# Seven down products spread over two pairs: order, leads and pages of a hand-planned transformer layer

## The chip, the cores and the metric

The kernel runs on one core of one Trainium2 chip. The metric is the device time in microseconds (us) of one execution, as the median of several runs.

## The reference

One layer of a streaming encoder on 512 tokens of width 1024, everything in float32:

```python
x = layer_norm(ALPHA * x + 0.5 * swiglu(x, ffn1_wg, ffn1_wu, ffn1_wd), ln1_g, ln1_b)     # D_FF = 2816
h = x @ w_in                       # q, k, v, indexer (qi, ki, wi), conv gates (bg, cg, u)
attn = dsa_attention(...)          # indexer scores, top 128 keys of each query, softmax with ALiBi over them
conv = bg * causal_dwconv3(cg * u)
x = layer_norm(ALPHA * x + concat(attn, conv) @ w_out, ln2_g, ln2_b)
x = layer_norm(ALPHA * x + 0.5 * swiglu(x, ffn2_wg, ffn2_wu, ffn2_wd), ln3_g, ln3_b)
x = x + sigmoid(x @ ple_gate_w) * (p @ ple_proj_w)

def swiglu(x, wg, wu, wd):
    return (silu(x @ wg) * (x @ wu)) @ wd
```

## The kernel before

**Numbers in two parts.** Every float32 operand of a matmul is split into a high part (a ScalarE cast, L115) and a low part (the rest, a VectorE subtraction, L116), and each product is made of three passes: high by high, high by low, low by high. For the weights of the down projection the low part is made otherwise (`Down.parts`): ScalarE writes the negated rounded value into the low page (L299), a DMA issued from GpSimd's queue adds the raw value to it in memory (L300), and ScalarE casts the high part (L301).

**Pairs.** The hidden width is 22 chunks of 128. In each FFN two chunks are computed plainly; the other twenty are taken two at a time as ten pairs (numbers 1 to 10) with a scheme of seven block products where the plain way has eight (`Two`, L426 to 481). Each product is 24 matmuls of 256 columns (L444). The operands of a pair are made in five steps of `weights` (L388): the load of four raw pages, A11, then S1/S2 (L403, L404), S3/S4 (L410, L411), and A12/A22 (`a2`). The products share two banks: x_ takes product 0, is copied out by ScalarE (L466) into a page `e`, and product 2 is then added onto the same bank; y_ likewise with product 1 (L468). At a pair's end its two chunks are split and summed by `pair_ops` (L269 to 282), whose sums go through the page `s_`.

**Down products.** Two pairs make a group of four chunks. A group's down projection is again seven block products (`Down`, L284 to 368) of 12 matmuls of 512 columns (L339), each with a weight operand of its own, made in this order by `prep`: B11, T1 = B12 - B11, T2 = B22 - T1, T3 = B22 - B12, B22, T4 = B21 - T2, B21. The differences are VectorE's (L305). The results are added into `nat` (L346). There are four such groups; the last six chunks go plainly (L586 to 597), fused with the norm.

**The order.** `order` lists the pair products and down products with an estimated duration (2.9 and 2.7 us), and `begin` lists the loads and preparations with a lead: each is called before the first product whose planned start is at or past the planned start of its own product less the lead. For a group, the down products are those of the pairs before it, and they stand behind certain of its pair products (L552, L553). A program that knows the dependences then orders each engine's queue by this program order and by readiness in a model of its own.

**Pages.** Nearly every operand lives in one of `NPAGES` SBUF pages of 4 KB per partition. `page()` takes the page that has been free longest, `free()` puts it at the end of the list. Both happen in program order; on the chip, the first instruction that writes a page waits for the last one that used it under its former owner, DMAs included.

**Middle.** After the first norm the value blocks (`v_proj`) are computed: the first `NV` at once, the others as fillers between the steps of the top-k search (`choose`). The ALiBi distances `dm` are made by GpSimd (L747, L748) and VectorE (L749).

Of the kernel before, what the change touches and what calls it, by code (L numbers as in the profile page):

```python
# [7 lines left out]
F32 = mybir.dt.float32  # L8
F32R = mybir.dt.float32r
AF = mybir.ActivationFunctionType  # L10
ALU = mybir.AluOpType

P = 128
# [3 lines left out]
NTB = S // P  # L17
# [8 lines left out]
BIG = 1.0e30  # L26
NEG = -1.0e38
REPL = -3.0e38

NPAGES = 41  # L30
BANKS = ((0, 1), (4, 5), (6,), (7, 2, 3))
AHEAD = 25
AHEAD_N = 150
# [2 lines left out]
AHEAD_D2 = 0  # L36


LEAD_L, LEAD_S, LEAD_DL, LEAD_DS = 16.0, 8.0, 18.0, 13.0
T_PLAIN, T_PAIR, T_DOWN = 11.5, 2.9, 2.7  # L40
NEMB = 2
AHEAD_P = 150
NV = 1
NQK = 3
NCH = 20
NPRE = 1
# [16 lines left out]
TOFF = (0, 128, 384, 768, 1280)  # L63
# [3 lines left out]
def layer_kernel(ctx: ExitStack, tc: tile.TileContext, x, ln1_g, ln1_b, ffn1_wg, ffn1_wu, ffn1_wd, w_in,  # L67
                 conv_w, w_out, ln2_g, ln2_b, ffn2_wg, ffn2_wu, ffn2_wd, ln3_g, ln3_b, ple_gate_w, ple_proj_w, x_t, p_t, out):
    nc = tc.nc
    sb = ctx.enter_context(tc.tile_pool(name="sb", bufs=1))  # L70
# [7 lines left out]
    def count(kind):  # L78
        counts[kind] = counts.get(kind, 0) + 1
        return counts[kind] - 1  # L80

    def ring(kind, n, shape, dt=F32):
        i = count(kind)
        return sb.tile(shape, dt, tag=f"{kind}{i % n}", name=f"{kind}_{i}")


    free_pages = list(range(NPAGES))
    owner = {}

    def page(shape, dt=F32R):  # L90
        i = free_pages.pop(0)
        t = sb.tile(shape, dt, tag=f"pg{i}", name=f"pg{i}_{count('pg')}")
        owner[id(t)] = (i, t)
        return t

    def free(*tiles):
        for t in tiles:
            free_pages.append(owner.pop(id(t))[0])
# [4 lines left out]
    def bank(group):  # L103
        g = GROUPS[group]
        return pp.tile([P, 512], F32, tag=f"bk{g[count('bank' + group) % len(g)]}", name=f"bk_{count('bank')}")
# [62 lines left out]
    def ts(t):  # L168
        return slice(t * P, (t + 1) * P)
# [78 lines left out]
    def ffn(X, wg, wu, wd, ln_g, ln_b, first, load_nat, groups, nplain, ahead, ahead_f, ahead_d):  # L248
# [249 lines left out]
        def add_down(f0, pairs):  # L498
            u = Down(f0, pairs)
            prods = u.products()  # L500
            loads = {0: ((0, 0),), 1: ((0, 1),), 2: ((1, 1),), 5: ((1, 0),)}
            for i in range(7):
                for at in loads.get(i, ()):
                    begin.append((LEAD_DL, len(order), lambda at=at: u.load(*at)))
                begin.append((LEAD_DS, len(order), lambda i=i: u.prep(i)))
                order.append((T_DOWN, lambda: next(prods)))
                yield
# [30 lines left out]
        def chain_pairs(pairs):  # L538
            for n in pairs:
                if n < 2 * n_down:  # L540
                    yield from add_pair(2 * n, lambda m, n=n: place_in(n, m), lambda n=n: ops[n // 2].append(pair_ops(pair_of[n])))
                else:
                    yield from add_pair(2 * n, lambda m, n=n: late_place(n, m), lambda n=n: late_done(n))
# [5 lines left out]
        for g in range(n_down):  # L549
            pairs = (2 * g + 2, 2 * g + 3) if g < n_down - 1 else (2 * g + 2, 2 * g + 3, 2 * g + 4)  # L550
            downs = add_down(4 * g, ops[g])
            for i, _ in enumerate(chain_pairs(pairs)):  # L552
                if i >= 2 and i % 3 != 1:  # L553
                    next(downs, None)
            for _ in downs:
                pass
# [75 lines left out]
    with tc.high_priority(offset=10000), tc.manual_schedule():  # L632
# [16 lines left out]
        ps = bank("all")  # L649
# [20 lines left out]
    def colT(u, group, tok0=0, m=P):  # L670

        ps = bank(group)
        mm(ps[:m, :S - tok0], [((u[0][:, c], u[1][:, c]), (x1T[0][:, c, tok0:], x1T[1][:, c, tok0:])) for c in range(NDC)])
        free(*u)
        return ps[:, :S - tok0]

    def col_unit(c0, ahead):
        return unit(rows(w_in[:, c0:c0 + P], 0, NDC), [P, NDC, P], ahead)


    v = []
    wv = [unit(rows(w_in[:, C_V:C_V + 512], c * P, 2), [P, 2, 512], AHEAD_V) for c in range(0, NDC, 2)]

    def v_proj(blocks):
        for t in blocks:
            ps = bank("main")
            mm(ps, [((x1T[0][:, c, ts(t)], x1T[1][:, c, ts(t)]), (wv[c // 2][0][:, c % 2], wv[c // 2][1][:, c % 2])) for c in range(NDC)])
            v.append(page([P, NH, 2, HD]))
            split(v[t][:, :, 0], v[t][:, :, 1], ps.rearrange("p (h d) -> p h d", h=NH))
            if t == NTB - 1:  # L690
                for u in wv:
                    free(*u)
            yield

    for _ in v_proj(range(NV)):
        pass
# [17 lines left out]
    def mm64(ps, q, e, at, k_hi, k_lo):  # L714

        nc.tensor.matmul(ps, lhsT=q[:, e, at], rhs=k_hi, start=True, stop=False)  # L716
        nc.tensor.matmul(ps, lhsT=q[:, e, at], rhs=k_lo, start=False, stop=True)  # L717
# [3 lines left out]
    ps = colT(u, "main", m=72)  # L721
# [12 lines left out]
    for j in range(4):  # L734
        ps = colT(col_unit(C_QI + j * P, AHEAD_I), "main", tok0=P)
# [2 lines left out]
        qi.append(t_)  # L738


    dm_pages = [page([P, 768], F32), page([P, 512], F32)]
    dm = [dm_pages[t // 3][:, TOFF[t % 3]:TOFF[t % 3] + (t + 1) * P] for t in range(NTB)]
    for t in range(NTB):
        w_ = (t + 1) * P
        d = dm[t]
        dn = ring("a", 2, [P, 512])
        nc.gpsimd.iota(d, pattern=[[1, w_]], base=-t * P, channel_multiplier=-1, allow_small_or_imprecise_dtypes=True)  # L747
        nc.gpsimd.tensor_scalar(dn[:, :w_], d, -1.0, None, op0=ALU.mult)  # L748
        nc.vector.tensor_tensor(d, d, dn[:, :w_], op=ALU.min)  # L749
    nc.vector.memset(dm[0][0:64, 64:128], -BIG)  # L750


    sc = {}
    for t in range(1, NTB):
        w_ = (t + 1) * P
        sc[t] = page([P, 512], F32)
        for h in (0, 2, 4, 6, 1, 3, 5, 7):
            ps = bank("sc")
# [10 lines left out]
    def choose():  # L769
        m8 = {t: ring("m8", 3, [P, 8]) for t in sc}  # L770
        for k in range(TOPK // 8):
            for t in sc:
                w_ = (t + 1) * P
                nc.vector.max(m8[t], sc[t][:, :w_])
            for t in sc:
                w_ = (t + 1) * P
                nc.vector.match_replace(sc[t][:, :w_], m8[t], sc[t][:, :w_], REPL)
            yield
        for t in sc:
            w_ = (t + 1) * P  # L780
            d = dm[t]
            nc.vector.tensor_scalar(sc[t][:, :w_], sc[t][:, :w_], REPL, -BIG, op0=ALU.not_equal, op1=ALU.mult)
            nc.vector.tensor_add(d, d, sc[t][:, :w_])
        free(*sc.values())
# [7 lines left out]
    def conv():  # L792
        for j in range(4):
            ps = colT(col_unit(C_CG + j * P, AHEAD_C), "main")
            z = page([P, 514], F32)
            nc.vector.memset(z[:, 0:2], 0.0)
            nc.scalar.copy(z[:, 2:], ps)
            yield
            ps = colT(col_unit(C_U + j * P, AHEAD_C), "main")
            nc.vector.tensor_mul(z[:, 2:], z[:, 2:], ps)  # L800
            y = ring("hf", 2, [P, 512])
            nc.scalar.activation(y, z[:, 0:512], AF.Copy, scale=cw[:, j, 0:1])
            for k in (1, 2):
                nc.vector.scalar_tensor_tensor(y, z[:, k:k + 512], cw[:, j, k:k + 1], y, op0=ALU.mult, op1=ALU.add)
            free(z)
            yield
            ps = colT(col_unit(C_BG + j * P, AHEAD_C), "main")
            nc.vector.tensor_mul(y, y, ps)
            t_ = page([P, 2, 512])
            split(t_[:, 0], t_[:, 1], y)  # L810
            convT.append(t_)
            yield
# [39 lines left out]
    def chain(*gens):  # L852
        for g in gens:
            yield from g

    def pull(g, n=1):
        for _ in range(n):
            next(g, None)

    ch = choose()  # L860
    fill = chain(v_proj(range(NV, NTB)), conv(), *[qk_proj(j, "main") for j in range(NQK)])
    done = 0
    for i in range(NTB - NV + 12 + 2 * NQK):
        while done < min(TOPK // 8 + 1, (i + 1) * (TOPK // 8 + 1) / NCH):
# [10 lines left out]
    def softmax(h):  # L875

        j, e = h // 2, h % 2
        slope = 2.0 ** -(h + 1)
        sp = [page([P, 768], F32), page([P, 512], F32)]
        a = [sp[t // 3][:, TOFF[t % 3]:TOFF[t % 3] + (t + 1) * P] for t in range(NTB)]  # L880
        soft[h] = a, sp
        st = ring("ss", 2, [P, NTB, 3])
        for t in range(NTB):
            w_ = (t + 1) * P
            ps = bank("qk")
            mm64(ps[:, :w_], qT[j], e, ts(t), kT[j][:, e, :w_], kL[j][:, e, :w_])
            nc.vector.tensor_tensor_reduce(a[t], ps[:, :w_], dm[t], -slope, 3.0e38, ALU.add, ALU.min, st[:, t, 0:1])
            nc.scalar.activation(a[t], a[t], AF.Exp, bias=st[:, t, 0:1], scale=-1.0, accum_out=st[:, t, 1:2])
            nc.vector.reciprocal(st[:, t, 2:3], st[:, t, 1:2])
            nc.vector.tensor_scalar(a[t], a[t], st[:, t, 2:3], None, op0=ALU.mult)  # L890
# [45 lines left out]
        if h % 2:  # L936
            free(qT[h // 2], kT[h // 2], kL[h // 2])
    pull(fill, 100)
    free(*v, *dm_pages)


    g_t, b_t = bcast(ln2_g[0]), bcast(ln2_b[0])
# [2 lines left out]
    for t in range(NTB):  # L945
        stats = ring("st", 4, [P, 2, 6])
        for half in range(2):
            hs = slice(half * 512, (half + 1) * 512)
            ps = bank(OB[t])
# [20 lines left out]
    for t in range(NTB):  # L970
# [3 lines left out]
        for half in range(2):  # L974
            cuts = (0, 512) if (t, half) != (NTB - 1, 1) else (0, 256, 512)
            for c0, c1 in zip(cuts, cuts[1:]):
                hs = slice(half * 512 + c0, half * 512 + c1)
                n = c1 - c0
                ps = bank("all")
# [34 lines left out]
```

## Time and profile before

| | |
|---|---|
| median of 3 runs | 1077.49 us |
| lowest and highest run | 1072.87 and 1077.82 us |
| the profiled execution | 1072.63 us |
| its span, first to last instruction | 1070.4 us |
| TensorE, matmuls | 1003.4 us busy, 94% of the span |
| VectorE | 838.8 us, 78% |
| ScalarE | 550.7 us, 51% |
| mean granted TensorE clock | 0.976 of full speed |

The span is that of the one execution that was profiled; durations and idle times below are of that execution. The first FFN lies at about 0 to 390 us, attention and conv from there to about 650, the second FFN to about 1027, and the last gate behind it.

### The profile page before, as it was taken

The page shows a single profiled execution, that of the slowest core. Times are in us where ns is not written, and L with a number is a line of the kernel's source. Part 1 is how long each engine was busy: PE and PEld are TensorE (multiplying, and loading weights), DVE is VectorE, ACT ScalarE, POOL GpSimd, SP SyncE. Part 2 cuts the span into 40 slices and gives each one's busy share as a digit, 9 for nine tenths or more (in the row PEclk, how much of TensorE's full clock was granted, in tenths as well). Part 3 has the DMA queues.
Part 4 walks back from the last instruction along what each step waited for, and adds up shares of the span by engine and source line. Part 5 has one row for each costly group of instructions (what it writes and reads, how often), then busy time and mean ns, then how long its engine had stood idle before and what let it go on. Part 6 is the DMA issues. An engine that isn't in the chain of part 4 may idle for free.

```text
span 1070.4 us, 15655 instructions
## 1 busy us (share of the span) xinstructions
PE 1003.4 (94%) x6215; PEld 896.3 (84%) x6215; DVE 838.8 (78%) x1321; ACT 550.7 (51%) x767; POOL 74.9 (7%) x91
## 2 busy tenths in 40 slices
PE   9997997979998989999999899997997979999998
PEld 7996996979998768888878779996996969988787
DVE  7986886778976866999479889976986778888742
ACT  6655654656655235422576835655654656656111
POOL 0010000100000120000000011000000100000100
PEclk9998998999999999999999999998998999999999
DMA  9575446745657112333102513475546744656121
GB/s 311 143 192 142 116 121 175 195 102 138 155 150 240 55 44 60 89 96 91 40 4 95 192 65 119 119 196 138 133 107 173 188 127 119 155 155 242 41 88 49
DMA packets 108824, 138.14 MB, mean 129 GB/s; under 512 B 6992, under 2 KB 83024, under 8 KB 108752
## 3 DMA queue, kind: packets, MB, share of 16 engines
q1 hardware_dynamic: 100688, 107.79, 31.9%
q0 software_dynamic: 8064, 29.36, 14.3%
q8 instruction: 48, 0.79, 0.3%
q14 instruction: 24, 0.20, 0.1%
HBM read 103.59 MB, written 4.19 MB: 101 GB/s over the span
## 4 chain that ended last, share of the span: by engine, by line
PE 50%; issue 24%; DMA 12%; DVE 8%; ACT 3%; POOL 2%; SPq 0%; POOLq 0%; DVEq 0%; ACTq 0%
PE bk L136 24%; PE bk L444 16%; PE bk L339 7%; DMA pg<-pg 6%; DVE pg L116 3%; DMA pg<-in_ffn_wg_dram 2%; ACT pg L115 2%; DMA pg<-in_ffn_wd_dram 2%; POOL pg L300 2%; DMA pg<-in_w_out_dram 1%; DVE nat L166 1%; PE bk L716 1%; POOL mv L164 1%; PE bk L150 1%; PE bk L717 1%
## 5 line engine op out<-in xcount | busy, mean ns | idle before, releaser
L115 ACT CAST pg<-pg 128x1024 fp32r<-128x1024 f32 (+2 forms) x270 | 254.3, 962 | 236.1 <-DVE pg L116 56.9
L116 DVE TENSOR_TENSOR pg<-pg,pg 128x1024 fp32r<-128x1024 f32 (+2 forms) x270 | 294.8, 1112 | 94.3 <-ACT pg L115 50.7
L444 PE MATMUL bk<-xq,pg 128*128 128x256 f32 x1920 | 244.8, 285 | 5.9 <-ACT pg L479 3.4
L444 PEld LDWEIGHTS bk<-xq,pg 128*128 128x128 f32 x1920 | 240.3, 193 | 11.3 <-ACT pg L479 3.8
L339 PE MATMUL bk<-pg,pg 128*128 128x512 f32 x672 | 176.3, 412 | 40.4 <-DMA pg<-pg 40.4
L339 PEld LDWEIGHTS bk<-pg,pg 128*128 128x128 f32 x672 | 130.1, 201 | 66.9 <-DMA pg<-pg 41.6
L444 PE MATMUL bk<-pg,pg 128*128 128x256 f32 x1440 | 184.1, 283 | 1.1 <-ACT pg L466 1.1
L444 PEld LDWEIGHTS bk<-pg,pg 128*128 128x128 f32 x1440 | 178.9, 192 | 3.6 <-ACT pg L466 1.5
L136 PE MATMUL bk<-pg,pg 128*128 128x512 f32 (+1 forms) x624 | 141.8, 378 | 3.5 <-DVE pg L116 1.7
L136 PE MATMUL bk<-xT,pg 128*128 128x512 f32 (+2 forms) x600 | 134.6, 384 | 0.2 <-ACT xT L115 0.2
L136 PEld LDWEIGHTS bk<-pg,pg 128*128 128x128 f32 x624 | 108.8, 188 | 24.8 <-DVE pg L116 2.5
L136 PEld LDWEIGHTS bk<-xT,pg 128*128 128x128 f32 (+1 forms) x600 | 110.7, 187 | 22.2 <-issue 1.3
L346 DVE SCALAR_TENSOR_TENSOR nat<-bk,nat 128x512 f32<-128x512 f32 x112 | 76.6, 687 | 20.5 <-PE bk L339 19.6
L300 POOL DMA_DIRECT2D pg<-pg x56 | 49.2, 878 | 536.7 <-ACT pg L299 336.0
L301 ACT CAST pg<-pg 128x1024 fp32r<-128x1024 f32 x56 | 58.3, 1045 | 33.8 <-PE bk L444 28.4
L136 PE MATMUL bk<-pg,xT 128*128 128x512 f32 (+1 forms) x312 | 69.3, 374 | 0.0
L299 ACT ACTIVATE pg<-pg 128x1024 fp32r<-128x1024 f32 x56 | 58.6, 1058 | 14.1 <-DVE pg L305 14.1
L136 PEld LDWEIGHTS bk<-pg,xT 128*128 128x128 f32 x312 | 55.1, 188 | 9.7
L164 POOL TENSOR_TENSOR mv<-mv,mhalf 128x1 f32<-128x1 f32 x12 | 18.0, 1497 | 408.9 <-DVE mv L163 408.9
L305 DVE TENSOR_TENSOR pg<-pg,pg 128x1024 f32<-128x1024 f32 x32 | 39.0, 1218 | 1.6 <-PE bk L444 1.5
L453 ACT ACTIVATE a<-pg 128x512 f32<-128x512 f32 x40 | 25.1, 627 | 26.8 <-DVE pg L476 26.8
L136 PEld LDWEIGHTS bk<-xq,pg 128*128 128x128 f32 x288 | 35.7, 192 | 3.7 <-ACT pg L115 1.6
(114 smaller groups left out, 864.1 us busy)
## 6 DMA issues: line engine op xcount, KB each, us to landing
pg<-pg POOLq DMA_DIRECT2D x56, 512.0 KB, 5.7
pg<-in_ffn_wd_dram SPq DMA_DIRECT2D x44, 512.0 KB, 4.6
pg<-in_ffn_wu_dram SPq DMA_DIRECT2D x43, 512.0 KB, 7.0
pg<-in_ffn_wg_dram SPq DMA_DIRECT2D x43, 512.0 KB, 4.8
pg<-in_w_in_dram SPq DMA_DIRECT2D x28, 512.0 KB, 3.6
pg<-in_w_out_dram SPq DMA_DIRECT2D x8, 512.0 KB, 3.9
pg<-in_ple_gate_w_dram SPq DMA_DIRECT2D x8, 512.0 KB, 4.2
pg<-in_x_t_dram SPq DMA_DIRECT2D x8, 256.0 KB, 5.9
```

The lines of the kernel that those rows point to most:

```text
L115: nc.scalar.copy(hi, src)
L116: nc.vector.tensor_sub(lo, src, hi.bitcast(F32))
L136: nc.tensor.matmul(ps, lhsT=st[a], rhs=mv[b], start=first and i == 0 and k == 0, stop=last and i == n - 1 and k == 2)
L164: nc.gpsimd.tensor_tensor(mv[:, 3:4], mv[:, 2:3], mhalf, op=ALU.pow)
L299: nc.scalar.mul(lo, src, -1.0)
L300: nc.gpsimd.dma_start(lo, src, accum_op=ALU.add)
L301: nc.scalar.copy(hi, src)
L305: nc.vector.tensor_sub(t, self.raw[a], self.raw[b])
L339: nc.tensor.matmul(banks[b], lhsT=st[x_][:, SLOT[a], ts(b)], rhs=w[y_][:, i], start=first and i == 0 and n == 0, stop=i == 1 and n == 2, s ...
L346: nc.vector.scalar_tensor_tensor(dst, banks[b], CY, dst, op0=ALU.mult, op1=ALU.add)
L444: nc.tensor.matmul(ps[:, i], lhsT=w[x_][:, c], rhs=X.q[b][y_][:, c], start=first and i == 0 and c == 0 and k == 0, stop=i == 1 and c == 3 ...
L453: nc.scalar.activation(s_t, e[:, :, 0], AF.Silu)
```

## The change

The down products no longer stand behind two of every three pair products but behind every second; the leads change (pair loads 16 to 14, down loads 18 to 22, down preparations 13 to 17; the pairs' other steps stay at 8); there is one page fewer, since `dm` gets a tile of its own (1280 columns) and gives back the two pages that it held from the indexer to the end of attention. `NV` becomes 2: the second value block is computed right behind the first norm, not as a filler.

```diff
-NPAGES = 41
+NPAGES = 40
...
-LEAD_L, LEAD_S, LEAD_DL, LEAD_DS = 16.0, 8.0, 18.0, 13.0
+LEAD_L, LEAD_S, LEAD_DL, LEAD_DS = 14.0, 8.0, 22.0, 17.0
 T_PLAIN, T_PAIR, T_DOWN = 11.5, 2.9, 2.7
...
-NV = 1
+NV = 2
...
             for i, _ in enumerate(chain_pairs(pairs)):
-                if i >= 2 and i % 3 != 1:
+                if i >= 2 and i % 2 == 0:
                     next(downs, None)
             for _ in downs:
                 pass
...
-    dm_pages = [page([P, 768], F32), page([P, 512], F32)]
-    dm = [dm_pages[t // 3][:, TOFF[t % 3]:TOFF[t % 3] + (t + 1) * P] for t in range(NTB)]
+    dm = sb.tile([P, 1280], F32, name="dm")
     for t in range(NTB):
         w_ = (t + 1) * P
-        d = dm[t]
+        d = dm[:, TOFF[t]:TOFF[t + 1]]
...
-    nc.vector.memset(dm[0][0:64, 64:128], -BIG)
+    nc.vector.memset(dm[0:64, 64:128], -BIG)
...
-            d = dm[t]
+            d = dm[:, TOFF[t]:TOFF[t + 1]]
...
-            nc.vector.tensor_tensor_reduce(a[t], ps[:, :w_], dm[t], -slope, 3.0e38, ALU.add, ALU.min, st[:, t, 0:1])
+            nc.vector.tensor_tensor_reduce(a[t], ps[:, :w_], dm[:, TOFF[t]:TOFF[t + 1]], -slope, 3.0e38, ALU.add, ALU.min, st[:, t, 0:1])
...
-    free(*v, *dm_pages)
+    free(*v)
```

## Rows read from the trace of the kernel before

**Rows 1.** The page, busy time of two engines: us (share of the span) xinstructions.

```profile
PE 1003.4 (94%) x6215; PEld 896.3 (84%) x6215; DVE 838.8 (78%) x1321; ACT 550.7 (51%) x767; POOL 74.9 (7%) x91
```

**Rows 2.** Waits: engine, line, whom it waited for: us in total, times, longest.

```profile
PE bk L339 <- DMA pg<-pg: 40.4, 6, 7.1
```

**Rows 3.** Timeline of TensorE, 126 to 176 us: start, us, what [idle before <-releaser].

```profile
141.00 3.04 PE L444 MATMUL bk<-xq,pg 128*128 128x256 f32 x24
143.88 2.91 PE L339 MATMUL bk<-pg,pg 128*128 128x512 f32 x12
146.63 3.04 PE L444 MATMUL bk<-pg,pg 128*128 128x256 f32 x24
...
149.50 2.91 PE L339 MATMUL bk<-pg,pg 128*128 128x512 f32 x12
...
163.62 0.63 PE L339 MATMUL bk<-pg,pg 128*128 128x512 f32 x2
...
171.90 4.43 PE L339 MATMUL bk<-pg,pg 128*128 128x512 f32 x10 [6.50 <-DMA pg<-pg]
```

**Rows 4.** Windows: busy us (x) of PE, PEld, DVE, ACT, POOL; PEclk, DMA share, GB/s.

```profile
103.40:171.90 68.50, 62.00 (x421) 57.66 (x421) 52.52 (x73) 37.61 (x46) 6.09 (x7) 0.95 0.58 144
...
405.00:540.00 135.00, 134.84 (x616) 111.58 (x615) 110.13 (x240) 54.05 (x83) 0.00 (x0) 1.00 0.27 75
...
162.00:178.00 16.00, 9.50 (x52) 8.28 (x52) 7.36 (x9) 5.14 (x7) 1.73 (x2) 0.79 0.83 218
```

**Rows 5.** Timeline of the other engines and SP's queue, 146 to 176 us.

```profile
155.32 0.59 ACT L466 COPY pg<-bk 128x512 f32<-128x512 f32 x1 [0.93 <-PE bk L444]
...
157.33 1.22 DVE L305 TENSOR_TENSOR pg<-pg,pg 128x1024 f32<-128x1024 f32 x1
...
158.46 1.22 DVE L116 TENSOR_TENSOR pg<-pg,pg 128x1024 fp32r<-128x1024 f32 x1
...
160.04 0.92 SPq L394 DMA_DIRECT2D pg<-in_ffn_wg_dram  x2
...
160.58 2.01 ACT L299 ACTIVATE pg<-pg 128x1024 fp32r<-128x1024 f32 x2
...
162.05 1.81 POOL L300 DMA_DIRECT2D pg<-pg  x2 [17.96 <-ACT pg L299]
...
171.88 1.83 DVE L116 TENSOR_TENSOR pg<-pg,pg 128x1024 fp32r<-128x1024 f32 x2 [6.49 <-DMA pg<-pg]
```

**Rows 6.** Timelines of VectorE, GpSimd and TensorE, first FFN's last group, around T4.

```profile
287.86 1.22 DVE L305 TENSOR_TENSOR pg<-pg,pg 128x1024 f32<-128x1024 f32 x1
...
290.93 0.88 POOL L300 DMA_DIRECT2D pg<-pg  x1 [11.41 <-ACT pg L299]
...
300.19 2.91 PE L339 MATMUL bk<-pg,pg 128*128 128x512 f32 x12
```

**Rows 7.** DMA issues, first 142 to 156, then whole span: KB, us to landing.

```profile
pg<-pg POOLq DMA_DIRECT2D x1, 512.0 KB, 4.5
...
pg<-in_ffn_wd_dram SPq DMA_DIRECT2D x44, 512.0 KB, 4.6
```

**Rows 8.** Timeline at the first norm's last block, 376 to 400 us.

```profile
380.26 5.60 PE L136 MATMUL bk<-pg,xT 128*128 128x512 f32 x24
...
382.00 0.95 DVE L749 TENSOR_TENSOR pg<-pg,a 128x384 f32<-128x384 f32 x1 [0.47 <-POOL a L748]
...
389.36 1.09 PE L150 MATMUL bk<-ident,nat 128*128 128x128 f32 x8 [3.50 <-DVE nat L166]
...
390.69 9.18 PE L136 MATMUL bk<-xT,pg 128*72 128x512 f32 x34 [0.24 <-ACT xT L115]
```

## The prediction, made before the change was run

> **What bounds the kernel now.** First the page: TensorE is busy for 94% of the span, no other engine over 78% [rows 1]. So time is to be had where TensorE waits, and at its lowered clock. Second, the waits, longest first: of its 67 us without work, 40.4 lie in six waits of the down projection's matmuls (L339) for one kind of DMA, `pg<-pg`, the accumulating one of L300 that makes a low part [rows 2]. Third, the timeline around the second of the six. I call a group's pair products p0 to p6 (first pair) and q0 to q6 (second), its down products d0 to d6; the next group's are r0 and so on. The third line of [rows 3] is p6, the fourth d3, the last two d5. It multiplies by T4, starts at 163.62, stops after the matmuls that need only the high part, and goes on at 171.90, with its ten remaining matmuls in 4.43 us where twelve take 2.91 (d3). The windows say why: granted clock 0.79 over 16 us, so some of it at the lower level of 1.2 GHz [rows 4]. One group lasts 68.5 us [rows 4]; its work is 14 x 2.88 + 7 x 2.75 = 59.6 (starts in [rows 3]). The stall therefore costs 8.9 us, 6.7 of waiting and some 2.2 of clock, and six cost 53 us.
>
> Why is T4 late? Followed back through the other engines [rows 5]: its DMA leaves at 162.05 because its ScalarE multiply (L299) ran at 160.58, and that because the page for the low part came free at 159.68, at the end of the last pass of `pair_ops` for p6 (VectorE L116, 158.46 + 1.22). Pages are handed out first in, first out, so the owner before can be counted off the code: for T4's low part it is `s_`, the sums of the pair that ended with p6. In the last group of each FFN, where no `s_` exists, T4's DMA leaves at 290.93, 9.3 us before d5 at 300.19, and d5 does not wait [rows 6]. VectorE's stop at 171.88 [rows 5] also follows: the page it waits for (S3/S4) was T4's difference. And the five loads that left just before (the first two at 160.04 [rows 5]) make the DMA slow: alone such a DMA lands in 4.5 us [rows 7], here in 9.8.
>
> **The change, part by part.** *Work:* every instruction stays; order, leads and pages change. The loads' own leads cost nothing: a load leaves when its page comes free, not when planned (the loads at 160.04 [rows 5] stood in the plan behind d5, which starts at 163.62 [rows 3]; their pages were last read by d4).
>
> *Plan of a group.* Adding up the planner's costs (2.9 and 2.7, which the starts in [rows 3] bear out) from p0 = 0: before, p6 25.5, d3 28.4, q0 31.1, d4 36.9, d5 42.5; after, p6 22.8, d2 25.7, q0 28.4, q1 31.3, d3 34.2, q2 36.9, q3 39.8, d4 42.7, q4 45.4, q5 48.3, d5 51.2, q6 53.9, d6 56.8. T4's lead before d5 grows from an effective 11.4 to 14 to 17, and its pages now come from the S3/S4 step of the second pair. The old stall goes. But a page fewer, held 4 us longer, shifts every page. I counted all of them off in both plans (after, the list runs down to none free). Three new links matter:
> (a) B22's low part (for d4) now gets `s_`, in the first three groups of each FFN.
> (b) In groups two and three, the first page of the second pair's `e`, into which L466 empties q0's bank, was B22's raw page, which B22's DMA reads. q2 adds into that bank, so q2 waits for that DMA.
> (c) In group one the raw page of B21 is that same B22 page, so B21's fetch, and T4 = B21 - T2, wait for it; and the `a2` page of the second pair, which q5 needs, was T4's difference.
>
> *Price of (b).* p6 ends at 25.7. To the end of `pair_ops`: before, 159.68 - 149.50 = 10.2 [rows 3, 5], of which 1.2 was T4's difference, no longer in between: 8.9 to 10.2, I take 9.5. To the DMA's issue: 162.05 - 159.68 = 2.4, of which 0.9 was another cast: 1.5 to 2.4, I take 1.9. Landing: 4.5 to 9.8 [rows 5, 7]; B21's fetch is over by then and the next pair's loads wait for pages that q2 itself frees, so it is nearest to the lone one: 5.0. L466: 0.59 [rows 5], with a semaphore on either side 0.85 (q0 ends at 149.50 + 2.75 + 2.88 = 155.13, the copy starts 0.19 later). Sum 17.25, so q2 starts at 42.95, not 36.9: 6.05 us. In that hole TensorE has d4's two high-part matmuls (0.47) and q3 (2.88, operands from 37 to 40, its bank emptied); left are 2.7 us in pieces under 2 us, at which I expect no clock loss. T4's DMA is then pushed by L466 and meets the loads: 1.1 more before d5. Together 3.8 us; ends: 15.75 - 11.2 - 3.35 = 1.2, and 23.3 - 11.2 = 12.1 without the fill, plus 2.2 of clock, 14.3. The bands of such a DMA decide it.
>
> One rule of the Trainium skill bears on this term ("DMA: Bandwidth & Descriptors", section "Anatomy of one DMA — SWDGE (gpsimd) path"): a DMA issued from GpSimd takes some 2.0 us plus its bytes at 436 GB/s, an estimate of 3.2 us for 512 KB. The lone one here took 4.5, so I keep the row; by the page the sum would be about 11 us lower (1.8 us at six places).
>
> *Price of (a) and (c), group one.* B22 lands at 25.7 + 9.5 + 1.9 + 5.0 = 42.1; with the loads at q2's end 43.0: d4 hardly waits. B21's fetch 4.6 (the median [rows 7]): 47.6. T4's difference to its DMA: 3.1 (287.86 to 290.93, pages free) to 4.7 (157.33 to 162.05), I take 3.3 [rows 5, 6]: 50.9; landing 5.0: 55.9. Meanwhile TensorE does d4, q4, half of q5, half of q6, and d5's first matmuls, to 51.7: 4.2 us idle, plus clock 2.2 = 6.4. Ends: 0 to 14.
>
> *T1, now due 17.2.* B12's page is freed when the last q6's chunk is put, an estimate of 3.7 us after its end at -2.7 (copy, Silu and product at 0.6 to 0.7 each and their queues): 1.0; load 4.6, difference to DMA 3.3, landing 5: 14. Three us spare: nothing.
>
> Two FFNs: 2 x (6.4 + 2 x 3.8) = 28 us where 53 were.
>
> *Second value block at the first norm, and `dm` in its own tile.* While the last block is normalised TensorE stands for 3.5 us before its transposes and 0.24 after, and the 34 matmuls that follow take 9.18, some 1.4 over 34 x 2.75 / 12 [rows 8]. The 24 matmuls of block 1 (5.6 us, as block 0's [rows 8]) fill it. They go from a stretch with TensorE fully busy [rows 4], which shortens by as much. `dm`'s four VectorE passes, one of them within the last block's chain at 382.00 [rows 8], no longer wait for pages. Gain 0 to 5.1; I take 5, as nothing else is late there.
>
> *Sum*, against the profiled execution (1072.6, span 1070.4 and 2.2 around it): 1072.6 - 53 + 28 - 5 = 1042.6. The runs shown have a median of 1077.5, 4.9 above that execution; half of this carried over, 1045.
>
> **The rivals.**
> *Same (chance 0.18):* the waits only move. For it: (a) hands the same late page to another operand. If groups two and three lose 9 as before, the sum is 1072.6 - 53 + 2 x (6.4 + 18) - 5 = 1063, and with 3 us more in group one 1069. The Trainium skill has a rule for this: "Perfetto Trace Analysis", section "Optimization Strategy", reads a gap that repeats as too little SBUF for the next tile; here that page count even falls by one. The trace agrees as to the cause: the gap comes six times, each behind a page.
> *Slower (0.16):* B22's DMA is late. Every us by which it lands after my 42.1 costs all six groups one: 6 us. At 30/6 = 5 us the gain is gone, at 6 it is slower by over 0.5%. For it: T4's landing of 9.8 alone would be 4.8 more. Against it: the loads that slowed T4 now come behind. With 9.8 and nothing filled: 4 x 15.4 + 2 x 14.4 = 90 for my 28, 1105.
> *All stalls gone (0.12):* `pair_ops` ends earlier and DMAs are hidden: 1072.6 - 53 - 5 = 1015. Against it: even the lower end of (b) holds q2 back.
>
> **How the numbers follow.** Forecast 0.54, its own range 1030 to 1062. The range: down to 1026 leaves out most of "all gone", up to 1075 most of "slower", together under 0.2. Half a per cent, some 5 us, is what the measurement can tell from no change. Faster: 0.54 + 0.12 + a third of "same" = 0.72; same the other two thirds and a little of "slower", 0.13; slower 0.15.
>
> **What would show it.** No wait of six or seven us at T4 in groups two and three; a shorter one there at a pair product (L444) behind ScalarE's L466, which waits for `pg<-pg`; in group one still a wait of L339 for `pg<-pg`; groups of 63 to 66 us for 68.5. No TensorE gap at the last block of the first norm. I am wrong if L339 waits for B22 as long as it did for T4, if TensorE's idle total stays near 67 us, or if a stall shows at an operand that I let pass (T1, the second pair's S1).

## The result: about half a per cent slower, and the profile after

Over fifteen runs of each kernel on one chip the changed kernel takes 1080.4 us (1076.7 to 1085.4), the kernel before 1074.5. The ratio is 1.0053, with a 95% interval of 1.0037 to 1.0068. The forecast was 1045 us, in a range up to 1075. The profiled execution took 1085.4, with a span of 1083.4 us, 13.0 more than before. It is the longest of its fifteen, and the 1072.6 profiled before lies below all fifteen of its own: the two profiles lie 12.8 us apart, the medians 5.9. The rows of this section are of these two profiles.

The page's busy row, for [rows 1], and the longest waits of TensorE, for [rows 2]:

```profile
PE 1009.0 (93%) x6215; PEld 901.2 (83%) x6215; DVE 838.4 (77%) x1321; ACT 551.7 (51%) x767; POOL 75.9 (7%) x91
```

```profile
PE bk L339 <- DMA pg<-pg: 20.5, 6, 6.3
PE bk L444 <- DVE pg L116: 12.3, 9, 2.2
PE bk L444 <- ACT pg L470: 11.0, 2, 5.5
...
PE bk L444 <- ACT pg L466: 3.6, 3, 1.7
```

The waits for the accumulating transfers are halved (40.4 to 20.5; the forecast had left 8.4, at T4 in group one). But others have come, L444 behind VectorE's L116 and ScalarE's L470: TensorE's idle total is 74.4 us where it was 67.0. The same 6,215 matmuls are busy 5.6 us longer, though the mean granted clock is no lower (0.980, before 0.976). Windows of the first FFN's four groups, each from its p0 to the next group's, the last to the plain down projection; first before, then after. The last row is the first row's group around d5.

```profile
52.28:120.94 68.66, 61.84 (x422) 57.68 (x421) 55.29 (x77) 38.08 (x48) 6.09 (x7) 0.95 0.59 146
120.94:189.34 68.40, 61.90 (x422) 57.58 (x421) 52.55 (x73) 37.61 (x47) 6.07 (x7) 0.95 0.59 147
189.34:257.51 68.17, 61.99 (x423) 57.69 (x421) 52.62 (x73) 37.72 (x47) 6.08 (x7) 0.95 0.58 147
257.51:343.28 85.77, 82.08 (x590) 77.90 (x589) 69.59 (x90) 51.13 (x65) 5.23 (x6) 0.98 0.62 170
```

```profile
52.09:126.30 74.21, 63.85 (x423) 58.44 (x421) 51.95 (x73) 38.84 (x49) 6.09 (x7) 0.95 0.52 128
126.30:189.99 63.69, 61.64 (x422) 57.18 (x421) 51.38 (x72) 36.91 (x46) 6.07 (x7) 0.97 0.60 154
189.99:257.52 67.53, 61.83 (x421) 57.50 (x420) 53.19 (x74) 38.02 (x47) 6.08 (x7) 0.97 0.59 151
257.52:350.82 93.30, 84.82 (x590) 80.42 (x588) 72.01 (x94) 51.24 (x64) 5.93 (x8) 0.95 0.59 165
...
110.00:124.00 14.00, 8.49 (x36) 7.36 (x37) 5.07 (x7) 4.36 (x5) 0.88 (x1) 0.76 0.56 135
```

Groups two and three became shorter, group one and the last longer. The second FFN repeats it: 72.1, 66.9, 61.6 and 92.9 us.

Group one, timelines of SP, VectorE, GpSimd and TensorE:

```profile
99.26 0.37 SPq L293 DMA_DIRECT2D pg<-in_ffn_wd_dram  x1
...
103.25 1.23 DVE L305 TENSOR_TENSOR pg<-pg,pg 128x1024 f32<-128x1024 f32 x1 [1.84 <-DMA pg<-in_ffn_wd_dram]
...
93.39 0.87 POOL L300 DMA_DIRECT2D pg<-pg  x1 [19.38 <-ACT pg L299]
...
106.55 0.86 POOL L300 DMA_DIRECT2D pg<-pg  x1 [1.03 <-ACT pg L299]
...
115.51 3.78 PE L339 MATMUL bk<-pg,pg 128*128 128x512 f32 x8 [5.91 <-DMA pg<-pg]
```

That is link (c): B21's fetch (99.26) leaves when B22's transfer (93.39) has landed, T4's difference waits for the fetch, and d5 waits 5.9 us for T4's transfer, which leaves at 106.55 and lands 9.0 us later.

The last group, timelines of SP, VectorE, GpSimd, ScalarE and TensorE, where [rows 6] showed no wait:

```profile
292.94 0.37 SPq L293 DMA_DIRECT2D pg<-in_ffn_wd_dram  x1
...
297.29 1.22 DVE L305 TENSOR_TENSOR pg<-pg,pg 128x1024 f32<-128x1024 f32 x1 [2.53 <-DMA pg<-in_ffn_wd_dram]
...
300.01 0.88 POOL L300 DMA_DIRECT2D pg<-pg  x1 [10.91 <-ACT pg L299]
...
308.53 1.04 ACT L301 CAST pg<-pg 128x1024 fp32r<-128x1024 f32 x1 [7.02 <-DMA pg<-pg]
309.48 0.58 ACT L470 COPY pg<-bk 128x512 f32<-128x512 f32 x1
...
310.11 5.49 PE L444 MATMUL bk<-pg,pg 128*128 128x256 f32 x24 [5.46 <-ACT pg L470]
```

B21's high part (L301) has got the page of T4's raw difference. ScalarE stands 7.0 us until T4's transfer, which leaves at 300.01, has read it; behind it in the queue stands L470, which empties a products' bank, and TensorE waits 5.5 us for that. Its next 24 matmuls take 5.49 us, where 3.04 is usual. This link I had not priced.

### The profile page after: what moved, and what is told of

Its sections match the earlier page's. It is cut to its first block, busy times and chain, and to the rows that moved or that the text cites. A ratio compares the mean times of both kernels' runs of the same rounds, so it can differ in the third digit from the quotient of the medians.

```text
span 1083.4 us, 15679 instructions
## 1 busy us (share of the span) xinstructions
PE 1009.0 (93%) x6215; PEld 901.2 (83%) x6215; DVE 838.4 (77%) x1321; ACT 551.7 (51%) x767; POOL 75.9 (7%) x91
## 3 DMA queue, kind: packets, MB, share of 16 engines
q0 software_dynamic: 8064, 29.36, 14.6%
## 5 line engine op out<-in xcount | busy, mean ns | idle before, releaser
L116 DVE TENSOR_TENSOR pg<-pg,pg 128x1024 fp32r<-128x1024 f32 (+2 forms) x270 | 296.4, 1111 | 113.4 <-ACT pg L115 71.5
L115 ACT CAST pg<-pg 128x1024 fp32r<-128x1024 f32 (+2 forms) x270 | 253.9, 961 | 212.3 <-DMA pg<-in_ffn_wu_dram 37.1
L444 PE MATMUL bk<-xq,pg 128*128 128x256 f32 x1920 | 245.5, 284 | 16.4 <-DVE pg L116 12.3
L444 PEld LDWEIGHTS bk<-xq,pg 128*128 128x128 f32 x1920 | 239.3, 192 | 22.8 <-DVE pg L116 14.4
L444 PE MATMUL bk<-pg,pg 128*128 128x256 f32 x1440 | 191.7, 291 | 17.4 <-ACT pg L470 11.0
L444 PEld LDWEIGHTS bk<-pg,pg 128*128 128x128 f32 x1440 | 186.8, 200 | 21.5 <-ACT pg L470 11.8
L339 PE MATMUL bk<-pg,pg 128*128 128x512 f32 x672 | 173.1, 404 | 20.8 <-DMA pg<-pg 20.5
L339 PEld LDWEIGHTS bk<-pg,pg 128*128 128x128 f32 x672 | 126.0, 195 | 46.9 <-DMA pg<-pg 23.6
L136 PE MATMUL bk<-pg,pg 128*128 128x512 f32 (+1 forms) x624 | 143.3, 380 | 6.5 <-ACT pg L115 5.4
L136 PEld LDWEIGHTS bk<-pg,pg 128*128 128x128 f32 x624 | 109.7, 190 | 28.8 <-ACT pg L115 6.6
L136 PE MATMUL bk<-xT,pg 128*128 128x512 f32 (+2 forms) x600 | 132.7, 381 | 0.0
L136 PEld LDWEIGHTS bk<-xT,pg 128*128 128x128 f32 (+1 forms) x600 | 110.0, 186 | 20.7
L346 DVE SCALAR_TENSOR_TENSOR nat<-bk,nat 128x512 f32<-128x512 f32 x112 | 75.3, 684 | 17.5 <-PE bk L339 17.5
L136 PE MATMUL bk<-pg,xT 128*128 128x512 f32 (+1 forms) x312 | 69.5, 374 | 0.0
L301 ACT CAST pg<-pg 128x1024 fp32r<-128x1024 f32 x56 | 58.1, 1037 | 16.4 <-DMA pg<-pg 15.2
L136 PEld LDWEIGHTS bk<-pg,xT 128*128 128x128 f32 x312 | 55.1, 188 | 9.8
L453 ACT ACTIVATE a<-pg 128x512 f32<-128x512 f32 x40 | 25.2, 631 | 59.7 <-DVE pg L476 59.5
L305 DVE TENSOR_TENSOR pg<-pg,pg 128x1024 f32<-128x1024 f32 x32 | 39.0, 1220 | 14.1 <-DMA pg<-in_ffn_wd_dram 13.4
L136 PE MATMUL bk<-xq,pg 128*128 128x256 f32 x288 | 39.5, 294 | 2.0 <-DVE xq L209 0.8
```

What stands on the lines that cost most here:

```text
L115: nc.scalar.copy(hi, src)
L116: nc.vector.tensor_sub(lo, src, hi.bitcast(F32))
L136: nc.tensor.matmul(ps, lhsT=st[a], rhs=mv[b], start=first and i == 0 and k == 0, stop=last and i == n - 1 and k == 2)
L301: nc.scalar.copy(hi, src)
L305: nc.vector.tensor_sub(t, self.raw[a], self.raw[b])
L339: nc.tensor.matmul(banks[b], lhsT=st[x_][:, SLOT[a], ts(b)], rhs=w[y_][:, i], start=first and i == 0 and n == 0, stop=i == 1 and n == 2, s ...
```

## The experiments

Two theories stood at the start. The first: the page links move the stalls, and what the change loses hangs on a few of them. The rival: the new order, or the two other parts of the change, cost the time whatever the pages.

Each comparison is with the kernel before on the same chip; the ratio has its 95% interval. The chips differ: the kernel before has medians of 1073.0 to 1076.7 us on them, so where two runs come from two chips, the difference of their ratios is the better measure. The table gives the eight groups of a profile, from the ScalarE copy that empties p0's bank (L466) to the next group's, the last to the third pair's L479.

| kernel | first FFN | second FFN |
|---|---|---|
| before | 69.8, 68.4, 68.2, 81.7 | 70.1, 68.8, 68.7, 79.7 |
| changed | 75.2, 65.8, 66.8, 87.2 | 73.3, 67.6, 62.8, 88.0 |
| plan_alone | 67.1, 70.3, 70.1, 89.3 | 65.4, 68.4, 71.4, 89.1 |
| leads_alone | 59.4, 64.2, 67.3, 83.8 | 59.5, 62.0, 64.9, 83.6 |
| leads_40 | 71.2, 68.5, 66.3, 86.2 | 63.7, 69.0, 66.3, 85.2 |
| last_high | 74.8, 66.6, 65.2, 79.6 | 72.7, 66.8, 62.3, 82.4 |
| first_raw | 72.6, 66.2, 67.6, 85.1 | 71.6, 64.7, 62.6, 88.7 |
| after_late | 62.5, 61.7, 62.3, 84.8 | 61.9, 62.3, 62.1, 86.8 |
| before_late | 66.7, 66.0, 63.8, 77.4 | 66.9, 65.0, 63.9, 78.1 |

### One link broken at a time

```diff
+    def turn():
+        free_pages.append(free_pages.pop(0))
...
         elif i == 6:
+            if self.f0 == 12:
+                turn()
             self.parts("B21")
```

> The changed kernel, except that in the last group of each FFN the first free page is put behind the others just before B21's two parts are taken, so that the high part no longer gets the page of T4's raw difference. All instructions and their order are the same. Theory (ScalarE waits in its queue for the accumulating transfer of T4's low part, and the copy that empties a products' bank waits behind it): the 7.0 us wait of L301 and the 5.5 us wait of TensorE on L470 go, the last group of each FFN is 5 to 8 us shorter; d5 may then wait for T4 itself for 1 to 4 us: 1068 us, 1062 to 1074. Rival (density, or the transfers are late whatever the pages): within 3 us of the changed kernel.

Measured: 1071.1 us, 0.9965 (0.9949 to 0.9982), 9.2 us below the changed kernel. ScalarE's queue after it:

```profile
299.65 1.04 ACT L305 CAST pg<-pg 128x1024 fp32r<-128x1024 f32 x1
300.58 0.58 ACT L476 COPY pg<-bk 128x512 f32<-128x512 f32 x1
```

The cast (now L305) runs at once and the copy (L476) behind it; the last groups are 7.6 and 5.6 us shorter. This one link cost about 9 us, as the theory had it.

The next run adds the turn before B21's load (`load` of (1, 0), `f0 == 12`).

> As the run before, and in the last group the free list is also turned by one just before B21's raw page is taken, so that it gets a page of T2's parts instead of B22's raw page; the low part of the second pair's last sums gets B22's. Theory: the load of B21 leaves about 5 us earlier, so T4 and its transfer are 4 to 5 us earlier and d5 waits for nothing: 3 to 6 us less than the run before, 1064 us, 1058 to 1070. Rival (the load's turn on SP or the five loads beside it set T4's time, not the page): the same as the run before, within 2 us.

Measured: 1071.8 us, 0.9966 (0.9949 to 0.9983): the rival, no change from the run before. B21's load was not what TensorE waited for there.

The same turn before B21's load, in the first group only (`f0 == 0`), without the others:

> The changed kernel, except that in the first group of each FFN the free list is turned by one just before B21's raw page is taken, so that it gets a page of the second pair's first operand, freed by its first product, instead of B22's raw page, which the accumulating transfer still reads. Theory (that page makes the fetch of B21 leave 6 to 9 us late, and with it T4, d5 and the rest): the 5.9 and 6.3 us stalls before d5 of these two groups go, and each is 6 to 7 us shorter: 1067 us, 1061 to 1073. Rival (T4 is late because of VectorE's and ScalarE's queues, or the five loads beside the fetch): the first groups keep 72 us or more, 1077 to 1083.

Measured: 1082.7 us, 1.0082 (1.0055 to 1.0109): no gain. VectorE and ScalarE in it:

```profile
98.45 1.23 DVE L119 TENSOR_TENSOR pg<-pg,pg 128x1024 fp32r<-128x1024 f32 x1 [3.73 <-DMA pg<-pg]
99.71 1.23 DVE L311 TENSOR_TENSOR pg<-pg,pg 128x1024 f32<-128x1024 f32 x1
...
110.14 1.04 ACT L118 CAST pg<-pg 128x1024 fp32r<-128x1024 f32 x1 [4.19 <-DMA pg<-pg]
```

T4's difference (L311) runs 3.5 us earlier and d5 no longer waits, but another split on VectorE now has B22's raw page (3.7 us), and a cast on ScalarE waits 4.2 us for a page that T4's transfer reads. The group is 2.6 us shorter (1.7 in the second FFN), not 7. Under this dealing the late pages went to other operands.

All three turns:

> The changed kernel with the turn in the first group (the run before) and both turns in the last group (last_both). Theory: the two gains add: 1058 us, 1052 to 1065. Rival (time won in the first groups is lost to the next late operand, the second pair's sums on VectorE): 1066 to 1072.

Measured: 1070.0 us, 0.9981 (0.9958 to 1.0003): as last_both, the rival.

### The parts alone

New order and new leads on the kernel before; then the changed kernel with both undone; then each alone:

```diff
-LEAD_L, LEAD_S, LEAD_DL, LEAD_DS = 16.0, 8.0, 18.0, 13.0
+LEAD_L, LEAD_S, LEAD_DL, LEAD_DS = 14.0, 8.0, 22.0, 17.0
...
-                if i >= 2 and i % 3 != 1:
+                if i >= 2 and i % 2 == 0:
```

> The kernel before with the new order (one down product behind every two products of the pairs) and the four new leads, and nothing else: 41 pages, the distances in two pages, one value block in the first norm. With 41 pages the list of free pages deals other pages: B21's raw operand gets a page of T2's operands in groups one to three, T4's low part the raw page of the up weights, and only in the last group does a part of B21 (now the low one) still get the page of T4's raw difference. Theory (the page links move the stall): group one takes 66 to 68 us instead of 74.2 and 72.1, the last group still waits on ScalarE; the first norm's 3.5 us are lost: 1065 us, 1058 to 1072. Rival (seven down products in fourteen pairs' products are too dense for the operand work, whatever the pages): group one and the last group are as long as in the changed kernel, 1080 to 1090.

Measured: 1086.1 us, 1.0111 (1.0090 to 1.0132), a time in the rival's range, with the rival's long last groups (89.3 and 89.1). The first groups are short, as the theory had it (67.1 and 65.4 us), but groups two and three are longer than before in three of four places: d1 now waits 3.3 to 4.4 us for a transfer there and in the last groups. Counted again, T1's difference has in them the page of the sums of the pair before, a link that the expectation had left out.

> The changed kernel with the old order and the old leads: 40 pages, the distances in a tile of their own, two value blocks in the first norm. Theory: the page of the products' sums now goes to T4's high part instead of the low one, so the stall before d5 stays in six groups, about as long; the first norm and the middle gain 3 to 4 us, the head of the second FFN loses nothing: 1071 us, 1066 to 1076. Rival (the 4.7 us that the head of the second FFN lost come from the value block or the page count): 1073 to 1080, with that head at 60 us or more.

Measured: 1069.6 us, 0.9948 (0.9930 to 0.9967): the time is as expected; the stalls before d5 are 3.5 to 5.5 us. But the head of the second FFN, from the norm's first transposes (L205) to p0, lasts 60.2 us, which is the rival's sign. It lasts 59.3 to 63.8 us in every run with 40 or 39 pages and 56.4 to 57.4 in every run with 41. Since the run leads_39 below, with no tile for the distances and one value block, has 59.3, the 3 to 7 us above the 56.5 of the kernel before go with the page count.

> The kernel before with the four new leads alone: the old order (a down product behind two of every three of the pairs' products), 41 pages, one value block in the first norm. T4 is now prepared ahead of the first pair's sums in groups two and three (its difference is issued before them on VectorE), and its low part gets a page freed two products earlier. Theory (what the change gains comes from the leads, what it loses comes from the denser order, in which no time is left between the late operands): the stall of 6 to 7 us before d5 goes in six groups and the last groups stay at 80 to 82 us: 1033 us, 1022 to 1045. Rival (an earlier start only moves the waits: B22's raw page and the page of the first sums stall the next fetch or the second pair's first copies): 1060 to 1075.

Measured: 1046.2 us, 0.9761 (0.9733 to 0.9788), a gain of 27 us, 1 us above the theory's range and far below the rival's; no matmul of L339 waits a microsecond for a transfer. (The expectations of this run and of plan_alone call the new order denser. It is the more spread one: down products behind products 3, 5, 7, ... where the old one ends after 12.)

> The kernel before with the new order alone: 41 pages, old leads. Counted off the code three pages are left at the worst place. Theory A (too few pages): with pages to spare the order costs little, 1066 to 1076. Theory B (the order itself): B22's and T4's operands are now prepared in the second pair, behind the first pair's sums on VectorE and beside the second pair's loads, and the parts of B21 get the pages of T2's and T4's raw differences: 1078 to 1095.

Measured: 1063.2 us, 0.9888 (0.9868 to 0.9908), faster than either theory allowed. So the order alone gains 11 us, the leads alone 27, both together lose 11. Neither part "is" the loss.

### One page fewer, two pages fewer

The changed kernel with the old order; and leads_alone with `NPAGES = 39`:

> The changed kernel with the old order of the products alone (down products behind products 3, 4, 6, 7, 9, 10 and 12 of a group's fourteen, counted from 1, where the changed kernel has 3, 5, 7, 9, 11, 13 and 14: the new order is the more spread one, not the denser one as the expectations above have it). New leads, 40 pages, distances in a tile, two value blocks. Theory (the leads gain, the new order loses more): the 27 us of the leads alone and some 5 us of the other parts add: 1042 us, 1036 to 1049. Rival (the leads need the 41st page: with 40 the raw page of B22 stands before T4's difference in the first group and T4's difference before the second pair's first copies): 1055 or more, first groups of 65 us or more.

Measured: 1073.8 us, 0.9994 (0.9973 to 1.0014): the rival, with first groups of 71.2 and 63.7 us. TensorE's longest waits in it are for VectorE (16.8 us of L444 behind L474, 13.6 of L339 behind L346), none for a transfer. Whether late pages lie behind them was not tested.

> The run leads_alone with 39 pages instead of 41 and nothing else. Counted off the code, the free list then runs as empty as in the changed kernel: none left at the worst place, 7.8 left on average (changed kernel 7.7, leads_alone 9.8), 159 of 318 pages taken within 6 us of the planner's time after they were given back (changed kernel 153, leads_alone 108). Theory A (the spread order hurts because it keeps operands longer and leaves too few pages): most of the loss appears here too, 1065 to 1085. Theory B (it hurts by where it puts the late operands, whatever the number of pages): 1044 to 1056.

Measured: 1079.7 us, 1.0042 (1.0027 to 1.0056): theory A. With order and leads fixed, 41, 40 and 39 pages give 1046, 1074 and 1080 us (the run with 40 also has the tile of the distances and the second value block). The 41st page, which the change gives away for that tile, is worth some 25 us here by the ratios. The Trainium skill's "Perfetto Trace Analysis", section "Optimization Strategy", names too little SBUF for the next tile as a possible cause of a gap that repeats. The next runs show that here it isn't the room alone.

### The same pages, dealt otherwise

```diff
     owner = {}
+    taken, later = [0], []
...
     def page(shape, dt=F32R):
+        taken[0] += 1
+        while later and (later[0][0] <= taken[0] or not free_pages):
+            free_pages.append(later.pop(0)[1])
         i = free_pages.pop(0)
...
+    def free_late(*tiles):
+        for t in tiles:
+            later.append((taken[0] + 10, owner.pop(id(t))[0]))
...
-        free(pair, s_)
+        free_late(pair, s_)
...
-            free(*[self.raw.pop(n) for n in names])
+            free_late(*[self.raw.pop(n) for n in names])
```

> The changed kernel with another dealing of its 40 pages, and nothing else: raw down operands, their differences, the chunk pair and its sums are given back to the free list only after ten more pages have been taken (or when the list is empty). Counted off the code, late pages taken again within 6 us of the planner's time fall from 27 to about 8 to 13, but other pages are taken again sooner (within 6 us: 126 to about 165 of 318). Theory 2 (the dealing sets the loss): 1050 to 1068. Theory 1 (too few pages): 1076 to 1095.

Measured: 1044.3 us, 0.9698 (0.9673 to 0.9723), faster than either theory allowed: 36 us below the changed kernel, with its order, leads and 40 pages. Its longest waits of TensorE, and windows of its groups one to three:

```profile
PE bk L144 <- ACT pg L123: 6.0, 5, 3.9
PE bk L452 <- DVE pg L124: 5.4, 13, 0.9
```

```profile
51.90:113.40 61.50, 60.40 (x423) 56.23 (x423) 49.78 (x70) 38.15 (x48) 6.10 (x7) 1.00 0.58 150
113.40:176.00 62.60, 61.45 (x429) 57.06 (x428) 53.24 (x74) 38.01 (x47) 6.07 (x7) 1.00 0.65 163
176.00:238.00 62.00, 60.57 (x420) 55.86 (x420) 52.12 (x73) 37.87 (x46) 6.08 (x7) 1.00 0.64 162
```

No wait for a transfer is left among the longest, the three groups stand 2 to 3 us above their work of 59.6, and the granted clock is 1.00 where it was 0.95 to 0.97. The gain lies in groups one to three: the last groups, at 84.8 and 86.8, gained 3.6 us together, where last_high took off 13.2.

> The run leads_40 with the same late dealing (ten takes). Late pages taken again within 6 us: from 25 to about 13; other pages: 110 to about 137. Theory 2: 1046 to 1060. Theory 1: 1070 to 1085.

Measured: 1084.1 us, 1.0069 (1.0052 to 1.0087): theory 1, 8 us slower than leads_40 by the ratios (10 by the medians).

> The run order_alone (new order, old leads, 41 pages) with late pages given back after twelve takes. Late pages taken again within 6 us: from 19 to 3; other pages: 80 to 112; one page is left at the worst place. Theory 2: 1035 to 1052. Theory 1 (the list runs thinner): 1060 to 1075.

Measured: 1046.9 us, 0.9719 (0.9695 to 0.9742): theory 2.

> The run leads_alone (old order, new leads, 41 pages) with late pages given back after ten takes. Late pages taken again within 6 us: from 24 to about 10; other pages: 84 to about 113. Theory 2: 1030 to 1045. Theory 1: 1048 to 1065.

Measured: 1060.1 us, 0.9850 (0.9828 to 0.9871): theory 1, 10 us slower than leads_alone by the ratios (14 by the medians). To give late pages back later is no rule: it made two kernels slower.

> The kernel before with late pages given back after ten more takes, nothing else. Counted off the code, T4's parts then get T3's pages, but T4's difference gets B22's raw page, and it still stands behind the first pair's sums in VectorE's queue. Theory (the gain needs the order or the leads: T4 is prepared behind the sums whatever page it gets): the stall before d5 stays at 4 us or more in six groups, 1062 to 1078. Rival (the dealing is the whole gain): 1040 to 1052.

Measured: 1046.5 us, 0.9748 (0.9716 to 0.9780): the rival. The dealing alone gives the kernel before 28 us, with its order and leads. VectorE in it, at the place of [rows 5]:

```profile
144.22 1.23 DVE L313 TENSOR_TENSOR pg<-pg,pg 128x1024 f32<-128x1024 f32 x1 [5.28 <-DMA pg<-in_ffn_wd_dram]
...
148.56 0.41 DVE L285 TENSOR_TENSOR pg<-pg 128x256 f32<-128x256 f32 x1
...
155.85 0.41 DVE L286 TENSOR_TENSOR pg<-pg,pg 128x256 f32<-128x256 f32 x1
```

T4's difference (L313) stands ahead of the pair's sums (L283 to L286). Before, it stood behind them, at 157.33 [rows 5]. My expectation took its place in the queue as given by the code's order. It is not: which page an instruction gets also changes where it is placed.

> The run plan_alone (new order and new leads, 41 pages, one value block, distances in pages) with late pages given back after twelve takes. Late pages taken again within 6 us: from 18 to 3. Theory (the dealing made plan_alone slow, and once it is right the order, the leads and the 41st page add little to each other): 1086 falls to 1038 to 1050. Rival (new order and new leads hold too many pages at once): 1060 or more.

Measured: 1067.2 us, 0.9935 (0.9910 to 0.9959): 19 us faster than plan_alone, but slower than either part alone with the late dealing, and in the rival's range. The theory fails: even with this dealing the order and the leads do not go together.

### The first norm

rest_alone and leads_40 with `NV = 1`:

> The run rest_alone with one value block in the first norm again: what is left of the change is the page count (40) and the tile for the distances. Theory (the second value block fills the 3.5 us gap of the first norm, and as much is lost later, where the output projection's last weights are split 4.2 us late behind a weight of the second FFN on ScalarE): the gap of 3.5 us is back, the later wait falls to 1.5 us as before, and the time is that of rest_alone within 2 us. Rival (the later wait belongs to the page count): both waits are there, 3 to 4 us more than rest_alone.

Measured: 1067.2 us, 0.9959 (0.9939 to 0.9979), the same as rest_alone. The gap of 3.50 us [rows 8] is gone with one value block too. GpSimd's passes for the distances, before and in this run, then TensorE at this run's last block:

```profile
377.06 0.54 POOL L747 IOTA pg<- 128x128 f32 x2 [2.84 <-PE bk L136]
...
380.19 3.24 POOL L748 TENSOR_SCALAR a<-pg 128x384 f32<-128x384 f32 x2
```

```profile
337.55 4.08 POOL L747 TENSOR_SCALAR a<-dm 128x256 f32<-128x256 f32 x3 [0.98 <-DVE hf L454]
...
378.53 1.10 PE L150 MATMUL bk<-ident,nat 128*128 128x128 f32 x8 [0.30 <-DVE nat L166]
...
601.55 0.76 PE L136 MATMUL bk<-pg,pg 128*128 128x512 f32 x2 [3.81 <-ACT pg L115]
```

In a tile of their own the distances are computed 40 us earlier, out of the norm's way, and that alone closes the gap: leads_39, with fewer pages and no tile, still has 2.5 us there. But the later wait of L136 (3.8 us, where 1.49 at most stood before in that stretch) is there too.

> The run leads_40 with one value block in the first norm. Theory (the tile for the distances has emptied VectorE's queue in the last block of the norm, so no gap is left for the second value block to fill): the same as leads_40 or up to 3 us faster. Rival (the second block still fills some of it): 2 to 5 us slower.

Measured: 1074.2 us, 1.0000 (0.9985 to 1.0014), the same as leads_40. The second value block is worth nothing in this kernel and the one above.

## Why the prediction was wrong, point by point

**The old stall goes.** Right. Its page `s_` no longer reaches T4. (One reading on the way was loose: of the five loads beside T4's transfer four left before it, the fifth 0.5 us after, and B21's accumulating transfer left behind it too.)

**(b), groups two and three.** Right in size, partly by luck: 63.7, 67.5, 66.9 and 61.6, mean 64.9, for 63.4. The page link is there: in all four groups the copy of q0's bank (L466) waits for `pg<-pg`, 1.3 to 3.1 us. But TensorE does not wait for that copy; the three waits of L444 behind L466 (3.6 us in all) lie at a group's first pair, two of them in the last groups. What it lost instead, in group two (161 and 162) and group three:

```profile
161.29 1.52 PE L444 MATMUL bk<-xq,pg 128*128 128x256 f32 x10 [1.90 <-DVE pg L116]
162.61 4.47 PE L339 MATMUL bk<-pg,pg 128*128 128x512 f32 x12
...
237.05 1.60 PE L339 MATMUL bk<-pg,pg 128*128 128x512 f32 x4 [2.35 <-DMA pg<-pg]
...
237.08 0.59 ACT L466 COPY pg<-bk 128x512 f32<-128x512 f32 x1 [1.91 <-DMA pg<-pg]
```

It waits for the same transfer at d4 (237.05; 2.4, 3.5 and 1.7 us in three of the four groups), which (a) had at nearly nothing. In three of the four it waits 1.7 to 1.9 us within q1 (161.29, its last ten matmuls), for VectorE's split of the second pair's S1, an operand that I had let pass and had named as a sign of being wrong. And I expected no loss of clock: the granted clock is 0.97 in three of the four windows, and twelve matmuls of d3 take 4.47 us for 2.91.

**(c), group one.** The mechanism was right, two terms too small. B22's transfer left at 41.3 us from p0 (93.39 - 52.09), where I had 37.1, and T4's landed in 9.0, where I took 5.0. TensorE also waits 3.7 us in this group for splits (L115, L116), for which I had no term. The group was priced at 66.0 and took 74.2 and 72.1: 14.3 us in all. That breaking the link gives back 2.6 says that the price does not belong to that one page. Nor does it belong to the shortage alone: after_late, with as few pages, has this group at 61.5.

**"Two FFNs: 2 x (6.4 + 2 x 3.8) = 28 us where 53 were."** This is the step that failed: the sum has no term for the last group, which it put at nothing without a reason, and prices group one at 6.4 where it cost 14.6 and 12.5. The last group's links had shifted too; 93.3 and 92.9 us against 85.8 and, by the starts in the trace, 83.5, 16.9 in all, of which last_high gives back 13.2 (9 of the whole time).

**First norm.** The gap went, but by the tile and not by the second block, and the 5 us did not arrive: the wait of L136 and the head of the second FFN, 4.8 us longer, took them. Outside the eight groups the execution is 2.1 us longer, not 5 shorter: 7.1.

With these the sum closes for the profiled pair. The old stalls had cost 54.5 rather than 53 (28.1 in the second FFN), so 1042.6 - 1.5 + 14.3 + 6.0 (4 x 1.5) + 16.9 + 7.1 = 1085.4, which the execution took. The medians lie 7 us closer together than this pair; which terms were smaller in the other executions, no trace shows.

**The rivals.** "Same", that the waits only move, was the nearest; I gave it 0.18 and ended it at 1069, since it had no new waits in the last group either.

**What I did not see at all.** I priced links one by one in an order taken as fixed. The runs show the dealing as a whole to be a lever as large as the rest: with first-in-first-out dealing the order and the leads gave -11, -27 and together +11 us, the late dealing by itself gave the kernel before -28 and the changed one -36; over all runs, which change nothing of the work, the time spans 1044 to 1086. Laid side by side by source line, the instruction lists of after_late and the changed kernel, whose only difference is the dealing, have 272 of VectorE's 1,321 instructions and 860 of TensorE's 6,215 in other places. In last_high, 27 and 3 moved (its expectation says none), so its 9 us are mostly a wait removed.

**What stays open.** How much of the 36 us in after_late is waits for pages and how much the other order of the queues was not separated. (Between the two profiles 32 us are idle time of TensorE, 74.4 to 42.4, and 9 are busy time of its matmuls, at a mean granted clock of 0.980 and 0.992.) Nor is it settled why the late dealing slows the old order with new leads (8 and 10 us by the ratios) while it speeds up the others: TensorE's longest waits there are for VectorE or ScalarE, not for a transfer. The lateness, ten or twelve takes, was not varied within a kernel, and last_high's turn was not tried together with the late dealing.

## What to carry to other kernels

Where tiles come from a list of free pages, the list is part of the schedule: an edit to an order, a lead or the number of pages deals every page anew, and the new owners can cost more than the edit gains. Count them off for all stages, the last and shortest included, and test the dealing by itself before crediting an order: here it gave 28 us with nothing else changed. When a change bundles edits, run each alone; gains of 11 and 27 us added up to a loss of 11.

## What the runs showed of the hardware

One cast that waits 7.0 us for a transfer at the head of ScalarE's queue costs TensorE 5.5 us through a bank copy that has nothing to do with it, and then 2.4 more, since the next 24 matmuls take 5.49 us for 3.04 (granted clock 0.79 over the 16 us around, below). T4's accumulating transfer in group one landed in 9.0 us with loads and a second such transfer beside it, against 4.5 for one alone [rows 7].

```profile
306.00:322.00 16.00, 11.89 (x66) 11.40 (x67) 11.39 (x18) 5.20 (x7) 0.00 (x0) 0.79 0.22 44
```
